# The order of three matmuls in a split-precision product with activations as stationary operand

## The chip, the cores and the metric

The kernel runs on one core of a Trainium2 chip. The metric is the device time of one execution in microseconds; the kernel before has a median of 1224.03 us over three runs.

## The reference

Two layers work on 512 tokens of width 1,024. The first mixes tokens by attention with forget gates, the second by a gated short convolution. Each is followed by an MLP with squared ReLU of width 4,096 and by a gated embedding. Everything is in 32-bit floats.

```python
for i in range(DEPTH):                                   # DEPTH = 2
    hn = rmsnorm(x, g[0])
    m = fox_attention(hn, ...) if i % 2 == 0 else short_conv(hn, ...)
    x = x + rmsnorm(m, g[1])
    f = jnp.square(jax.nn.relu(rmsnorm(x, g[2]) @ w_mlp_up[i])) @ w_mlp_down[i]
    x = x + rmsnorm(f, g[3])
    gate = jax.nn.sigmoid(rmsnorm(x, g[4]) @ w_ple_gate[i])
    x = x + rmsnorm((p[i] @ w_ple_proj[i]) * gate, g[5])
```

## The kernel before

TensorE multiplies in a reduced 32-bit format. To keep the precision, each operand is split in two parts: a high part (`hi`, a cast on ScalarE, line 272) and a low part (`lo`, the source less the high part, on VectorE or GpSimd, line 273). A product a x b is then three matmuls into the same PSUM bank: high by high, and the two mixed ones. The function `mm3` (line 262) issues them. Its first operand is the stationary one: it is loaded into the array ahead of each matmul. The second streams through, 512 columns at most. The reduction runs over blocks of 128 rows, so a bank gets a chain of such products; the first matmul of the chain clears the bank and the last one closes it.

Two kinds of calls exist. Where the result is to lie transposed (the projections `qk`, `up`, `u`, `c`, `b`), the weights are stationary and the tokens stream. Where it is to lie with tokens on the partitions, the activations of 128 tokens are stationary and 512 columns of weights stream. The second kind are the values `v`, the output projections `o` of attention and `co` of the convolution, the down projection `dn`, the gate `pg` and the embedding `pp`. `dn` sums its blocks in seven products per group by Strassen's scheme, with sums of activations (`A11`, `A12`, `S1`, `S3`, ...) as stationary operand.

Weights come from memory through 14 buffers (`raw`), fetched on SP's queue. `wide` returns the high and low part of a block and has up to eight further blocks prepared ahead, so `wh` and `wl` are normally ready long before their use. In names such as `wl_7264` the number tells one tile from the next. The activations' parts `hTh` and `hTl` are made after each norm: four transposes (`n_p`, line 320) into a bank, a cast to `hTh`, a subtraction to `hTl`. In the profile's rows a matmul reads out<-moving,stationary.

The order of instructions on each engine is set by a scheduler, which simulates the program and moves an instruction ahead where another would wait; at the start, at the end of attention and in the very last block some engines have an order by hand. Engines run their queues in order.

Of the kernel before, what the change touches and what calls it, by code (L numbers as in the profile page):

```python
# [21 lines left out]
KT = D // P  # L22
# [46 lines left out]
def trunk(ctx: ExitStack, tc, x, pT, g, wv, wqk, bf, wo, wci, wcq, cw, wco, wup, wdn, wpp, wpg, out):  # L69
    nc = tc.nc  # L70
# [122 lines left out]
    def wide(*key, soon=SOON):  # L193

        prepare(where[key] + 1 + soon)
        return ready[key]
# [62 lines left out]
        while any(k in keys for _, k, _ in later):  # L259
            later.pop(0)[2]()  # L260

    def mm3(ps, a, b, start, stop):

        nc.tensor.matmul(ps, a.hi, b.hi, start=start, stop=False)  # L264
        nc.tensor.matmul(ps, a.lo, b.hi, start=False, stop=False)  # L265
        nc.tensor.matmul(ps, a.hi, b.lo, start=False, stop=stop)  # L266
        streamed[0] += 3 * ps.shape[-1]
        due()

# [98 lines left out]
    def tokens_of(pair, t):  # L368
        return pair.at(lambda h: h[:, t * P : (t + 1) * P])

    def tokens(pair, k, t):
        return pair.at(lambda h: h[:, k, t * P : (t + 1) * P])

    def soon(t, n):

        return FEW if n else SOON

    def mixer_out(kind, lhs, xs, gB, then, opened):


        mgs, sums = {}, {}
        for t, n in BLOCKS:
            if (t, n) == (2, 0):
                prepare(where[kind, 1, KT - 1] + 1 + SOON)
            at = (t, n) in opened
            ps = opened.pop((t, n)) if at else bank(f"{kind}{n}_{t}")
            for k in range(KT - 1 if at else 0, KT):
                mm3(ps, lhs(k, t), wide(kind, n, k, soon=soon(t, n)), k == 0, k == KT - 1)
            sums[t, n] = squares(ps, f"{kind}s{n}_{t}")
            mgs[t, n] = gained(ps, gB, n, f"{kind}m{n}_{t}")  # L390
            if (t, 1 - n) in mgs:
                residual(t, *([d.pop((t, i)) for i in range(2)] for d in (mgs, sums)), xs[t],
                         f"{kind}r")
                then(t)

    def attention(hT, first_x, g0, b_f, work, by_hand):
# [47 lines left out]
        def values(c, t, mid=None):  # L444

            c0, width = V_CHUNKS[c]
            n_v = min(width, D - c0)
            ps = bank(f"v{c}_{t}")
            for k in range(KT):
                if width == 256:  # L450
                    w = wide("v", c, k // 2).at(lambda u: u[:, k % 2 * 256 : k % 2 * 256 + 256])
                else:
                    w = wide("v", c, k, soon=0 if mid else SOON)
                if not mid:
                    mm3(ps[:, :width], tokens(hT, k, t), w, k == 0, k == KT - 1)
            HH, LH, HL = ("hi", "hi"), ("lo", "hi"), ("hi", "lo")
            for n in range(2 if mid else 0):
                for part, of in (HH, HL, LH) if n == 0 else (HH, LH, HL):
                    if n and of == "lo":
                        mid()  # L460
                    for k in range(4 * n, 4 * n + 4):
                        nc.tensor.matmul(
                            ps[:, :width], getattr(tokens(hT, k, t), part),
                            getattr(ready["v", c, k], of),
                            start=k == 0 and part == of, stop=k == KT - 1 and of == "lo",
                        )

            def keep_v():
                if n_v < width:
                    nc.vector.tensor_tensor(  # L470
                        out=logit[:, t * H : (t + 1) * H], in0=ps[:, n_v:width], in1=b_f,
                        op=ALU.add,
                    )
                splits = []
                for c1 in range(0, n_v, 256):
                    src = ps[:, c1 : c1 + 256].rearrange("p (i e d) -> p i e d", e=2, d=HD)
                    block = vs[t][(c0 + c1) // 256].rearrange("p (i r) -> p i r", i=2)
                    for e in range(2):
                        hi = block[:, :, 192 * e : 192 * e + HD]
                        lo = block[:, :, 64 + 64 * e : 128 + 64 * e]  # L480
                        splits.append((hi, lo, src[:, :, e, :]))
                for hi, _, src in splits:
                    nc.scalar.copy(hi, src)
                for hi, lo, src in splits:
                    nc.vector.tensor_tensor(
                        out=lo, in0=src, in1=hi.bitcast(F32), op=ALU.subtract
                    )

            return keep_v
# [103 lines left out]
        banks_o = {}  # L593
        oT, complete, streaming = [], [], [True]
# [11 lines left out]
        def out_part(ts, ks):  # L606

            streaming.clear()
            split_o()
            for k in ks:  # L610
                for t in ts:
                    for n in range(2):
                        if (t, n) not in banks_o:
                            banks_o[t, n] = bank(f"o{n}_{t}")
                        w = wide("o", n, k, soon=O_SOON)
                        mm3(banks_o[t, n], tokens(oT[0], k, t), w, k == 0, False)
                        yield

        def stream():
# [29 lines left out]
        with tc.manual_schedule(engines={E.PE, E.DVE, E.Activation, E.Pool}):  # L649
# [3 lines left out]
            hs = scale_rows(0, r)  # L653
# [195 lines left out]
    def mlp(l, hT, xs, then, late):  # L849
# [45 lines left out]
        def down(gr, A):  # L895

            for i in STEPS:
                a_name, b_name = PRODUCTS[i]
                banks = [bank(f"dn{l}_{gr}_{i}{s}") for s in range(2)]
                for p in range(2):  # L900
                    w = wide("dn", l, gr, b_name, p)
                    for s in range(2):
                        mm3(
                            banks[s], A[a_name, p].at(lambda h: h[:, s * P : (s + 1) * P]), w,
                            p == 0, p == 1,
                        )
                for s in range(2):
                    if gr == 0:
                        acc[i, s] = page(f"acc{l}_{i}_{s}")
                        nc.scalar.copy(acc[i, s][:, :S], banks[s])  # L910
                    else:
                        a = acc[i, s][:, :S]
                        ins = nc.vector.tensor_tensor(out=a, in0=banks[s], in1=a, op=ALU.add)  # L913
                        if gr == 1:
                            tc.add_manual_dep(
                                ins.ins, lows[gr].ins.name,
                                mybir.DependencyInfo(
                                    mybir.DependencyClass.NoSync, mybir.DependencyReason.DATA
                                ),
                            )  # L920
# [25 lines left out]
        total, hs, gB = combine(), [], []  # L946
# [14 lines left out]
        for t in range(NB):  # L961
            banks = [bank(f"dn{l}_7_{t}_{n}") for n in range(2)]
            for f, n in [(f, n) for f in range(4) for n in range(2)] if t == 0 else [
                (f, n) for n in range(2) for f in range(4)
            ]:
                w = wide("dn", l, 7, n, f, soon=14)
                mm3(banks[n], tokens_of(hs[f], t), w, f == 0, f == 3)
            for n in range(2):
                a = total[t, n][:, :S]
                nc.vector.tensor_tensor(out=a, in0=banks[n], in1=a, op=ALU.add)  # L970
            fs = [total[t, n][:, :S] for n in range(2)]
            sums = [squares(f, f"fs{l}_{t}_{n}") for n, f in enumerate(fs)]
            mg = [gained(f, gB, n, None, total[t, n]) for n, f in enumerate(fs)]
            residual(t, mg, sums, xs[t], f"mr{l}")
            then(t)

    def ple(l, hT, xs, gB, then):
        def proj(t, n):
            pe = bank(f"pp{l}_{n}_{t}")
            for k in range(2):  # L980
                mm3(
                    pe, tokens_of(wide("p", l, k), t),
                    wide("pp", l, n, k), k == 0, k == 1,
                )
            return pe

        def last_block(t, n, gate, mg, q):
# [5 lines left out]
            for c, pe in zip(halves, pes):  # L993
                for k in range(2):
                    mm3(
                        pe[:, : S // 2], tokens_of(wide("p", l, k), t),
                        wide("pp", l, n, k).at(lambda w: w[:, c]), k == 0, k == 1,
                    )
            with tc.manual_schedule(engines={mybir.EngineType.DVE}):
                for i, (c, pe) in enumerate(zip(halves, pes)):  # L1000
# [13 lines left out]
                c = halves[1]  # L1014
# [24 lines left out]
        for t, n in BLOCKS:  # L1039
# [4 lines left out]
            ps = bank(f"pg{l}_{n}_{t}")  # L1044
            for k in range(KT):
                w = wide("pg", l, n, k, soon=soon(t, n))
                mm3(ps, tokens(hT, k, t), w, k == 0, k == KT - 1)
            gate = page(f"gate{l}_{n}_{t}")
            nc.scalar.activation(gate[:, :S], ps, AF.Sigmoid)
            if l == 1 and (t, n) == BLOCKS[-1]:  # L1050
# [42 lines left out]
    oT = lhs  # L1093
# [120 lines left out]
```

## Time and profile before

| | |
|---|---|
| three runs | 1223.32, 1224.03, 1225.0 us |
| the profiled execution | 1224.06 us, its span 1222.3 us |
| mean granted TensorE clock | 0.998 |
| TensorE busy | 1211.6 us (99%), 6,209 matmuls, as many loads of a stationary operand |
| VectorE, ScalarE, GpSimd busy | 913.6 (75%), 671.6 (55%), 666.0 us (54%) |

PE stands for the matmuls, PEld for the loads of the stationary operand, which run beside matmuls. A group's row gives line, engine, operation, operands and shape, the count, the busy time, the mean duration in ns and the idle time ahead. A row of the timeline gives the start, the duration and the same names. The printed ends of matmuls are modelled and overlap; the pace is read from the starts.

### The profile page before, as it was taken

What the parts mean: (1) busy time and instruction counts of PE and PEld (TensorE: products, weight loads), DVE (VectorE), ACT (ScalarE), POOL (GpSimd) and SP (SyncE); (2) the same over time, 40 slices, a digit from 0 to 9 for tenths busy, and PEclk for the clock granted to TensorE, in tenths of its full rate; (3) what the DMA queues carried; (4) which work ended last, traced back from release to release, by engine and by line L of the source; (5) the groups of instructions that cost most, each with busy time, mean ns of one, the idle gap of its engine ahead of it and who ended that gap; (6) DMA issues with size and microseconds to landing.
All of it is one profiled execution on the core that took longest, in us unless ns stands there. A gap on an engine that the chain in (4) does not pass through costs nothing.

```text
span 1222.3 us, 18723 instructions
## 1 busy us (share of the span) xinstructions
PE 1211.6 (99%) x6209; PEld 1033.0 (85%) x6209; DVE 913.6 (75%) x1420; ACT 671.6 (55%) x1421; POOL 666.0 (54%) x623
## 2 busy tenths in 40 slices
PE   9999999999999999999999999999999999999997
PEld 8888888898888888888889999989888888888886
DVE  6558888576769766879877798866776787669873
ACT  5457778558634563455565434445756345635551
POOL 5026667154887777775213255316677878778210
PEclk9999999999999999999999999999999999999999
DMA  8556554623244224428123033552422443235401
GB/s 275 156 154 164 167 146 127 207 87 104 79 137 127 90 70 128 138 80 291 64 91 114 19 103 98 162 172 70 138 79 61 137 138 98 66 114 182 163 14 56
DMA packets 86021, 148.73 MB, mean 122 GB/s; under 512 B 10082, under 2 KB 17810, under 8 KB 85924
## 3 DMA queue, kind: packets, MB, share of 16 engines
q1 hardware_dynamic: 85488, 147.01, 39.9%
q8 instruction: 49, 0.80, 0.3%
q10 hardware_dynamic: 436, 0.53, 0.1%
q14 instruction: 48, 0.39, 0.1%
HBM read 136.93 MB, written 6.37 MB: 117 GB/s over the span
## 4 chain that ended last, share of the span: by engine, by line
PE 94%; issue 2%; DVE 1%; ACT 1%; POOL 1%; DMA 0%; POOLq 0%; DVEq 0%; ACTq 0%
PE up L265 9%; PE up L266 9%; PE up L264 9%; PE dn L264 8%; PE dn L265 8%; PE dn L266 8%; PE qk L265 2%; PE qk L264 2%; PE qk L266 2%; PE pg L265 2%; PE pg L264 2%; PE pg L266 2%; PE pT L562 1%; PE n_p L320 1%; PE co L264 1%
## 5 line engine op out<-in xcount | busy, mean ns | idle before, releaser
L273 DVE TENSOR_TENSOR wl<-raw,wh 128x512 fp32r<-128x512 f32 (+1 forms) x387 | 377.2, 1018 | 14.7 <-ACT wh L272 13.3
L272 ACT CAST wh<-raw 128x512 fp32r<-128x512 f32 (+1 forms) x398 | 217.5, 620 | 4.6 <-DVE xd L356 4.4
L265 PE MATMUL up<-hTh,wl 128*128 128x512 f32 (+1 forms) x576 | 210.2, 365 | 0.0
L266 PE MATMUL up<-hTl,wh 128*128 128x512 f32 (+1 forms) x576 | 209.6, 365 | 0.0
L264 PE MATMUL up<-hTh,wh 128*128 128x512 f32 (+1 forms) x576 | 208.7, 366 | 0.0
L867 ACT ACTIVATE r<-up 128x512 f32<-128x512 f32 (+1 forms) x72 | 39.4, 547 | 203.9 <-PE up L266 191.1
L273 POOL TENSOR_TENSOR wl<-dn_T,wh 128x512 fp32r<-128x512 f32 x96 | 132.5, 1413 | 30.0 <-ACT wh L272 30.0
L167 POOL TENSOR_TENSOR dn_T<-raw,raw 128x512 f32<-128x512 f32 x56 | 86.4, 1553 | 70.1 <-DMA raw<-in_wdn 61.2
L265 PEld LDWEIGHTS up<-hTh,wl 128*128 128x128 f32 x576 | 108.6, 189 | 17.5
L264 PEld LDWEIGHTS up<-hTh,wh 128*128 128x128 f32 x576 | 108.6, 189 | 17.5
L266 PEld LDWEIGHTS up<-hTl,wh 128*128 128x128 f32 x576 | 108.3, 189 | 17.5
L913 DVE TENSOR_TENSOR acc<-dn,acc 128x512 f32<-128x512 f32 x168 | 107.4, 679 | 15.4 <-PE dn L266 15.4
L167 POOL TENSOR_TENSOR dn_T<-raw,dn_T 128x512 f32<-128x512 f32 x56 | 92.3, 1649 | 2.2
L272 ACT CAST wh<-dn_T 128x512 fp32r<-128x512 f32 x112 | 61.4, 616 | 11.0 <-POOL dn_T L167 11.0
L273 DVE TENSOR_TENSOR A12l<-q,A12h 128x512 fp32r<-128x512 f32 x28 | 22.5, 803 | 54.2 <-ACT A12h L272 54.2
L927 POOL TENSOR_TENSOR acc<-acc,acc 128x512 f32<-128x512 f32 x28 | 46.9, 1707 | 9.9 <-DVE acc L913 9.9
L265 PE MATMUL qk<-hTh,wl 128*128 128x512 f32 x128 | 51.0, 399 | 0.0
L266 PE MATMUL qk<-hTl,wh 128*128 128x512 f32 x128 | 51.0, 398 | 0.0
L264 PE MATMUL qk<-hTh,wh 128*128 128x512 f32 x128 | 50.9, 398 | 0.0
L265 PE MATMUL pg<-wh,hTl 128*128 128x512 f32 x128 | 50.5, 394 | 0.0
L264 PE MATMUL pg<-wh,hTh 128*128 128x512 f32 x128 | 50.4, 394 | 0.0
L266 PE MATMUL pg<-wl,hTh 128*128 128x512 f32 x128 | 50.1, 392 | 0.0
(403 smaller groups left out, 3213.4 us busy)
## 6 DMA issues: line engine op xcount, KB each, us to landing
raw<-in_wup SPq DMA_DIRECT2D x128, 256.0 KB, 2.8
raw<-in_wdn SPq DMA_DIRECT2D x128, 256.0 KB, 2.9
raw<-in_wcq SPq DMA_DIRECT2D x36, 256.0 KB, 3.0
raw<-in_wqk SPq DMA_DIRECT2D x32, 256.0 KB, 4.6
raw<-in_wpg SPq DMA_DIRECT2D x32, 256.0 KB, 4.1
g<-in_g SPq DMA_DIRECT2D x22, 256.0 KB, 5.5
prl<-neg_c SPq DMA_DIRECT2D x16, 256.0 KB, 6.8
raw<-in_wo SPq DMA_DIRECT2D x16, 256.0 KB, 3.3
```

What stands on the lines that cost most here:

```text
L167: ins = nc.gpsimd.tensor_tensor(out=B[name], in0=B[a], in1=B[b], op=op)
L264: nc.tensor.matmul(ps, a.hi, b.hi, start=start, stop=False)
L265: nc.tensor.matmul(ps, a.lo, b.hi, start=False, stop=False)
L266: nc.tensor.matmul(ps, a.hi, b.lo, start=False, stop=stop)
L272: nc.scalar.copy(hi, src)
L273: return eng.tensor_tensor(out=lo, in0=src, in1=hi.bitcast(F32), op=ALU.subtract)
L320: nc.tensor.transpose(ps[:, j * P : (j + 1) * P], h[:, j * P : (j + 1) * P], ident)
L562: nc.tensor.transpose(ps[:, b * P : (b + 1) * P], probs[h][b][:, j * P : (j + 1) * P], ident)
L867: nc.scalar.activation(r[:, :n], ps[:, :n], AF.Relu)
L913: ins = nc.vector.tensor_tensor(out=a, in0=banks[s], in1=a, op=ALU.add)
L927: nc.gpsimd.tensor_tensor(out=a, in0=a, in1=acc[i, s][:, :S], op=ALU.add)
```

## The change

The calls with activations as stationary operand pass a flag, and `mm3` then issues the two mixed products in the other order: the weights' low part second, with the stationary operand of the first matmul, and the activations' low part third. The calls with weights as stationary operand keep their order.

```diff
-    def mm3(ps, a, b, start, stop):
-
+    def mm3(ps, a, b, start, stop, turned=False):
+
+        last = (a.hi, b.lo), (a.lo, b.hi)
         nc.tensor.matmul(ps, a.hi, b.hi, start=start, stop=False)
-        nc.tensor.matmul(ps, a.lo, b.hi, start=False, stop=False)
-        nc.tensor.matmul(ps, a.hi, b.lo, start=False, stop=stop)
+        nc.tensor.matmul(ps, *last[not turned], start=False, stop=False)
+        nc.tensor.matmul(ps, *last[turned], start=False, stop=stop)
...
-                mm3(ps, lhs(k, t), wide(kind, n, k, soon=soon(t, n)), k == 0, k == KT - 1)
+                mm3(ps, lhs(k, t), wide(kind, n, k, soon=soon(t, n)), k == 0, k == KT - 1, True)
...
-                mm3(ps, tokens(hT, k, t), w, k == 0, k == KT - 1)
+                mm3(ps, tokens(hT, k, t), w, k == 0, k == KT - 1, True)
```

The same `True` is added to the calls for `v`, `o`, `dn` (twice) and `pp` (twice). The lines of the changed kernel stand one further down: 265, 266 and 267 for the three matmuls.

The first place is PE at the end of attention, where the output product of attention (`o`) is put between the products of the last heads (`ps_o`, `sc`). Before:

```order
L264 MATMUL o_0_2921<-wh_3086,hTh 128x512
L265 MATMUL o_0_2921<-wh_3086,hTl 128x512
L580 MATMUL ps_o_3134<-ph_0_3070,v_3_153 128x512
L581 MATMUL ps_o_3134<-pl_0_3071,v_3_153 128x512
L580 MATMUL ps_o_3134<-ph_1_3099,v_3_157 128x384
L266 MATMUL o_0_2921<-wl_3087,hTh 128x512
L546 MATMUL sc_2_3137<-kh_1_2621,qs_1_2620 128x384
```

The same place after the change:

```order
L265 MATMUL o_0_2921<-wh_3086,hTh 128x512
L581 MATMUL ps_o_3134<-ph_0_3070,v_3_153 128x512
L582 MATMUL ps_o_3134<-pl_0_3071,v_3_153 128x512
L581 MATMUL ps_o_3134<-ph_1_3099,v_3_157 128x384
L266 MATMUL o_0_2921<-wl_3087,hTh 128x512
L267 MATMUL o_0_2921<-wh_3086,hTl 128x512
L547 MATMUL sc_2_3137<-kh_1_2621,qs_1_2620 128x384
```

The three matmuls of attention still stand ahead of the one with `wl_3087`; the one with `hTl` has gone behind it.

The second place is PE in the gate product of the first layer, second column of weights, first block of tokens (`pg_1_0`). Before:

```order
L264 MATMUL pg_1_0_7395<-wh_7263,hTh 128x512
L265 MATMUL pg_1_0_7395<-wh_7263,hTl 128x512
L320 MATMUL n_p_0_7426<-ident,n_h_0_7199 128x128 x4
L266 MATMUL pg_1_0_7395<-wl_7264,hTh 128x512
L264 MATMUL pg_1_0_7395<-wh_7272,hTh 128x512
```

After:

```order
L265 MATMUL pg_1_0_7395<-wh_7263,hTh 128x512
L321 MATMUL n_p_0_7426<-ident,n_h_0_7199 128x128 x4
L266 MATMUL pg_1_0_7395<-wl_7264,hTh 128x512
L267 MATMUL pg_1_0_7395<-wh_7263,hTl 128x512
L265 MATMUL pg_1_0_7395<-wh_7272,hTh 128x512
```

The transposes follow the first matmul directly, and the one with `wl_7264` comes one matmul sooner. Some rows later the four transposes `n_p_1_7433` likewise move ahead of the matmul with `wl_7291`.

The third place is VectorE beside it. Before:

```order
L273 TENSOR_TENSOR wl_7264<-raw_7265,wh_7263 128x512
L273 TENSOR_TENSOR wl_7273<-raw_7274,wh_7272 128x512
L273 TENSOR_TENSOR wl_7282<-raw_7283,wh_7281 128x512
L273 TENSOR_TENSOR wl_7291<-raw_7292,wh_7290 128x512
L273 TENSOR_TENSOR hTl<-n_p_0_7426,hTh 128x4x128
L273 TENSOR_TENSOR wl_7300<-raw_7301,wh_7299 128x512
```

After:

```order
L274 TENSOR_TENSOR wl_7264<-raw_7265,wh_7263 128x512
L274 TENSOR_TENSOR wl_7273<-raw_7274,wh_7272 128x512
L274 TENSOR_TENSOR wl_7282<-raw_7283,wh_7281 128x512
L274 TENSOR_TENSOR hTl<-n_p_0_7426,hTh 128x4x128
L274 TENSOR_TENSOR wl_7291<-raw_7292,wh_7290 128x512
L274 TENSOR_TENSOR wl_7300<-raw_7301,wh_7299 128x512
```

The subtraction for `hTl` goes ahead of the one for `wl_7291`; the others keep their places.

More of the change, by code (lines that the diff above doesn't have):

```diff
@@ L454, in values @@
                 if not mid:
-                    mm3(ps[:, :width], tokens(hT, k, t), w, k == 0, k == KT - 1)
+                    mm3(ps[:, :width], tokens(hT, k, t), w, k == 0, k == KT - 1, True)
             HH, LH, HL = ("hi", "hi"), ("lo", "hi"), ("hi", "lo")
@@ L615, in out_part @@
                         w = wide("o", n, k, soon=O_SOON)
-                        mm3(banks_o[t, n], tokens(oT[0], k, t), w, k == 0, False)
+                        mm3(banks_o[t, n], tokens(oT[0], k, t), w, k == 0, False, True)
                         yield
@@ L904, in down @@
                             banks[s], A[a_name, p].at(lambda h: h[:, s * P : (s + 1) * P]), w,
-                            p == 0, p == 1,
+                            p == 0, p == 1, True,
                         )
@@ L966, in mlp @@
                 w = wide("dn", l, 7, n, f, soon=14)
-                mm3(banks[n], tokens_of(hs[f], t), w, f == 0, f == 3)
+                mm3(banks[n], tokens_of(hs[f], t), w, f == 0, f == 3, True)
             for n in range(2):
@@ L982, in proj @@
                     pe, tokens_of(wide("p", l, k), t),
-                    wide("pp", l, n, k), k == 0, k == 1,
+                    wide("pp", l, n, k), k == 0, k == 1, True,
                 )
@@ L996, in last_block @@
                         pe[:, : S // 2], tokens_of(wide("p", l, k), t),
-                        wide("pp", l, n, k).at(lambda w: w[:, c]), k == 0, k == 1,
+                        wide("pp", l, n, k).at(lambda w: w[:, c]), k == 0, k == 1, True,
                     )
```

## The prediction

> **What bounds the kernel now.** I read the page first: the engines' busy time, the clock over the slices and the chain of work that ended last.
>
> ```profile
> span 1222.3 us, 18723 instructions
> PE 1211.6 (99%) x6209; PEld 1033.0 (85%) x6209; DVE 913.6 (75%) x1420; ACT 671.6 (55%) x1421; POOL 666.0 (54%) x623
> PEclk9999999999999999999999999999999999999999
> PE 94%; issue 2%; DVE 1%; ACT 1%; POOL 1%; DMA 0%; POOLq 0%; DVEq 0%; ACTq 0%
> ```
>
> TensorE is busy in 99% of the span at full clock, and 94% of the chain lies on it. A busy PE is not yet a PE at its peak, so two questions follow: how far apart the matmuls start, and how long PE waits. The timeline of PE in a dense stretch of the MLP answers the first. The rows are the first and last of ten consecutive matmuls with 512 columns, and of seven with 256 columns.
>
> ```profile
> 300.47 0.39 PE L264 MATMUL up<-hTh,wh 128*128 128x512 f32 x1
> ...
> 302.51 0.39 PE L264 MATMUL up<-hTh,wh 128*128 128x512 f32 x1
> 279.55 0.28 PE L266 MATMUL up<-hTl,wh 128*128 128x256 f32 x1
> ...
> 280.27 0.28 PE L266 MATMUL up<-hTl,wh 128*128 128x256 f32 x1
> ```
>
> Nine steps in 2.04 us are 0.2267 us a matmul of 512 columns; six steps in 0.72 us are 0.120 us for 256. The second 256 columns cost 0.107 us, so about 0.013 us of each matmul (2 x 0.120 - 0.2267) does not depend on its width. The durations printed (0.39) overlap and say nothing of the pace. The view of waits, for PE alone, answers the second question.
>
> ```profile
> PE warm_p L1083 <- DVE warm L1066: 1.6, 1, 1.6
> PE ps_o L580 <- DVE pl L273: 0.9, 1, 0.9
> PE c L264 <- DVE za L803: 0.7, 1, 0.7
> PE pT L562 <- DVE pl L273: 0.6, 1, 0.6
> ```
>
> That is the whole answer: 3.8 us in four waits, none of them in a product that the change touches. `warm_p` is the start, `ps_o` and `pT` are attention's own, and `c` has the weights stationary. So the change works inside a stream that hardly ever stops. It can gain only by a faster pace, and lose by a new wait.
>
> **The change part by part.** Every product that is turned keeps its three matmuls, its operands and its sum in PSUM. Nothing is added or removed on any engine: 6,053 rows on PE, 1,403 on DVE, 1,256 on ACT, 621 on POOL and 613 on SP before and after. There are 774 turned products of 512 columns: 456 of `dn`, 128 of `pg`, 64 each of `o` and `co`, 32 of `v`, 30 of `pp`. Another 36 have 256 columns. Three things can differ.
>
> *The pace.* In a turned product the first two matmuls now share their stationary operand; before, they shared the moving one. The rows of two forms of `dn` show what the shared moving operand was worth, and the loads of a pair that already shares its stationary operand (`qs`, lines 546 and 547) show whether the second load is left out.
>
> ```profile
> L265 PE MATMUL dn<-wh,S3l 128*128 128x512 f32 x112 | 43.6, 389 | 0.0
> L266 PE MATMUL dn<-wl,S3h 128*128 128x512 f32 x112 | 40.0, 389 | 0.0
> L546 PEld LDWEIGHTS sc<-kh,qs 128*128 128x128 f32 x64 | 12.1, 189 | 2.0 <-DVE nmx L549 0.3 <-DVE pl L273 0.3
> L547 PEld LDWEIGHTS sc<-kl,qs 128*128 128x128 f32 x64 | 12.1, 188 | 1.3
> ```
>
> The second matmul of a `dn` product repeats the moving operand of the first, the third repeats neither: both have 389 ns. The 64 second matmuls on `qs` have 64 loads of their own, of 188 ns like every other. What such a pair costs in an undisturbed stretch is in the timeline at 79 us.
>
> ```profile
> 79.31 0.39 PE L266 MATMUL qk<-hTl,wh 128*128 128x512 f32 x1
> 79.55 0.39 PE L546 MATMUL sc<-kh,qs 128*128 128x512 f32 x1
> 79.55 0.19 PEld L547 LDWEIGHTS sc<-kl,qs 128*128 128x128 f32 x1
> 79.77 0.39 PE L547 MATMUL sc<-kl,qs 128*128 128x512 f32 x1
> 79.78 0.19 PEld L264 LDWEIGHTS qk<-hTh,wh 128*128 128x128 f32 x1
> 80.00 0.39 PE L264 MATMUL qk<-hTh,wh 128*128 128x512 f32 x1
> ```
>
> From the first `sc` matmul to the second, with the same stationary operand, it is 0.22 us; from the second to the `qk` matmul after it, with another one, 0.23. The load runs beside the matmul ahead of it, whatever it loads. I take 0.00 us a pair. The reading is good to 0.01 us, so the bound from these rows is 774 x 0.01 = 7.7 us either way; I put it among the rivals and not into the likeliest case, because the pair sits on the ordinary pace.
>
> The Trainium skill ("TensorE: Matmul & The Clock Gate", Part 2, on loading the stationary operand) speaks for a gain: the load is an instruction of its own so that one can load once and multiply repeatedly. The rows at 79 us disagree for this kernel: the load is issued again. By the rule the time would be that of the first rival below; by the rows the pace adds 0.
>
> *The wait for the weights' low part.* It is needed one matmul earlier, the activations' low part one later. In most places the weights are split far ahead. Two places are tight. The first is the end of attention, where VectorE makes the low part of the output weights (`wl_3087` of the order) just in time.
>
> ```profile
> 207.53 0.40 PE L265 MATMUL o<-wh,hTl 128*128 128x512 f32 x1
> 207.76 0.43 PE L580 MATMUL ps_o<-ph,v 128*128 128x512 f32 x1
> 208.03 0.40 PE L581 MATMUL ps_o<-pl,v 128*128 128x512 f32 x1
> 208.26 0.34 PE L580 MATMUL ps_o<-ph,v 128*128 128x384 f32 x1
> 208.44 0.39 PE L266 MATMUL o<-wl,hTh 128*128 128x512 f32 x1
> 207.55 0.69 DVE L273 TENSOR_TENSOR wl<-raw,wh 128x512 fp32r<-128x512 f32 x1
> ```
>
> The low part is done at 207.55 + 0.69 = 208.24. The new order keeps the three attention matmuls between the first and the second of this product; only the 0.23 us matmul at 207.53 goes from ahead of them to behind. So the waiting matmul comes up at 208.44 - 0.23 = 208.21: 0.03 us early. Behind it on PE wait the activations' low part, which is ready, and the next scores. Before, a gap of 0.20 us was enough, so the wait is between 0.03 and 0.23 us; I take 0.15. The later products of this kind have more room and are costed at nothing.
>
> The second place is the gate product of the second column (`pg_1_0`), in both layers, where VectorE works without a pause.
>
> ```profile
> 608.82 0.39 PE L265 MATMUL pg<-wh,hTl 128*128 128x512 f32 x1
> 609.05 0.60 PE L320 MATMUL n_p<-ident,n_h 128*128 128x128 f32 x4
> 609.40 0.47 PE L266 MATMUL pg<-wl,hTh 128*128 128x512 f32 x1
> ...
> 611.33 0.39 PE L265 MATMUL pg<-wh,hTl 128*128 128x512 f32 x1
> 607.93 2.49 DVE L273 TENSOR_TENSOR wl<-raw,wh 128x512 fp32r<-128x512 f32 x4
> 609.68 0.59 ACT L272 CAST hTh<-n_p 128x512 fp32r<-128x512 f32 x1 [0.31 <-PE n_p L320]
> 610.34 0.68 DVE L273 TENSOR_TENSOR hTl<-n_p,hTh 128x512 fp32r<-128x512 f32 x1
> 610.94 1.88 DVE L273 TENSOR_TENSOR wl<-raw,wh 128x512 fp32r<-128x512 f32 x3
> ```
>
> Four low parts in 2.49 us are 0.62 us each, so the first (`wl_7264`) is done at 608.55 and needed, after the move, at 609.40 - 0.23 = 609.17: 0.6 us to spare. The fourth (`wl_7291`) is done at 610.42; the new order puts the `hTl` of 0.68 us ahead of it, so it is done by 611.1. The order also puts four transposes (0.35 us, from 609.05 to 609.40 for such a group) ahead of its matmul, which then starts at 611.33 + 0.35 = 611.68: again 0.6 us to spare. Less is left if `hTl` has to wait for ScalarE's cast of the transposes, which ends 0.23 us sooner than before at best, at 609.68 + 0.59 - 0.23 = 610.04: then `wl_7291` ends at 610.04 + 0.68 + 0.62 = 611.34, 0.35 us ahead. I cost the place at nothing; its cover is these 0.35 to 0.6 us, twice in the run.
>
> *The stalls that are there.* The clearest in a turned product are in the first group of `dn`, by the timeline of PE.
>
> ```profile
> 285.63 0.39 PE L266 MATMUL dn<-wl,A12h 128*128 128x512 f32 x1
> 285.99 0.50 PE L264 MATMUL dn<-wh,S1h 128*128 128x512 f32 x1
> ...
> 287.29 0.40 PE L266 MATMUL dn<-wl,S1h 128*128 128x512 f32 x1
> 287.81 1.19 PE L264 MATMUL dn<-wh,A12h 128*128 128x512 f32 x4
> ```
>
> Against the pace they lose 0.36 - 0.23 = 0.13 and 0.52 - 0.23 = 0.29 us. Both fall on the first matmul of a product (line 264), which waits for a high part or a free bank, and the first stays first. Nothing is recovered: 0. The few swaps on DVE and ACT and one on SP follow the shifted matmuls by one or two instructions; the tightest of them is the `pg_1_0` case above.
>
> The sum is +0.15 us. The profiled execution took 1224.06 us, 1.8 more than its span; the median of the three runs is 1224.03. So **1224.2 us**: no change that can be measured, 0.2% (2.4 us) being about what a measurement of this kernel can tell from none.
>
> **The rivals.** *A shared stationary operand makes the pace faster.* If all of the 0.013 us that each matmul costs beyond its columns were the exchange of the stationary operand, and fell away where it stays, 774 + 36 products would save 810 x 0.013 = 10.5 us: 1213.7. For it: the change makes exactly such pairs in 810 places. Against it: the loads of `qs` are issued all the same, and the pair keeps the pace. Smaller gains down to 1221.6 belong here: 3% for the full effect, 5% for a part.
>
> *VectorE becomes the bound in the gate product (slower).* The low parts are now awaited one matmul sooner, with `hTl` ahead of one. The point from which it decides is 0.35 us of lateness. If two more VectorE operations than I count (2 x 0.62 us) fell ahead of the awaited low part, PE would stand 1.24 - 0.35 = 0.9 us a layer; with three, 1.5 us. Two layers and the 0.15 give 1226.0 and 1227.2. For it: VectorE has no pause from 607.93 to 612.82. Against it: the order moves one operation, not three. 7% for over 1226.5.
>
> *A wait that is there goes away (faster).* Transposes behind a product's first matmul start 0.23 us sooner and could shorten the 0.9 and 0.6 us that `ps_o` and `pT` wait in attention's end. If both vanished, 1224.2 - 1.5 = 1222.7, still within 0.2%. Against it: the 0.9 us falls at 219 us, after a stretch of PE work that is not shortened. 10%.
>
> **How the numbers follow.** The forecast has 75%; with the rival of 1222.7, 85% lie within 0.2%. Faster by more has 8% (the pace), slower by more 7% (VectorE). The range takes the bounds: below, 1.5 us of vanished waits and the 0.7 us by which the runs lay under their median (1223.32), 1224.2 - 2.2 = 1222.0; above, 0.08 us more at the end of attention, 0.9 us for one layer late by two operations and 1.0 us for the runs' spread upward (1225.0): 1226.2.
>
> **What would show it.** Right: PE's list of waits again holds these four, PE starts 512-column matmuls every 0.2267 us in `dn`, with as many loads as matmuls, and VectorE's low parts in `pg_1_0` end before their matmul. Wrong: fewer loads than matmuls, or a step under 0.22 us from the first to the second matmul of a turned product, or a PE wait for `wl` in `pg` or `o`.

## The result, and the profile after

The change makes the kernel slower by a little. Six runs after it took 1227.12 to 1229.44 us, median 1229.11; six of the kernel before on the same chip 1223.32 to 1225.0, median 1224.22. The ratio is 1.0037, with a 95% interval of 1.0026 to 1.0047: 4.9 us, outside the forecast range (1222.0 to 1226.2). The profiled execution took 1228.79 us.

The page of the profile after: the span, the engines and the chain.

```profile
span 1227.1 us, 18716 instructions
PE 1213.8 (99%) x6209; PEld 1032.9 (84%) x6209; DVE 917.4 (75%) x1420; ACT 671.6 (55%) x1421; POOL 669.5 (55%) x623
PE 89%; issue 3%; DVE 3%; ACT 2%; POOL 2%; DMA 0%; POOLq 0%; DVEq 0%; ACTq 0%
```

There are as many loads as matmuls, as before: no load is left out. But the chain lies on PE for 89% in place of 94%, and more of it on VectorE, ScalarE and GpSimd (1% each before). PE's waits after:

```profile
PE warm_p L1084 <- DVE warm L1067: 1.6, 1, 1.6
PE c L265 <- DVE za L804: 1.1, 1, 1.1
PE co L265 <- ACT wh L273: 1.1, 1, 1.1
PE ps_o L581 <- DVE pl L274: 0.9, 1, 0.9
PE c L266 <- DVE wl L274: 0.6, 1, 0.6
PE pT L563 <- DVE pl L274: 0.6, 1, 0.6
PE c L265 <- ACT wh L273: 0.2, 1, 0.2
```

Three are new, for a high or low part of weights, and none lies in `o` or `pg`. The list adds 2.3 us to the 3.8 of before, less than is lost. So I lined up the matmuls of the two traces by their place on PE and read how far the later one lags. The lag stays between 0.064 and 0.066 us from 300 to 595 us, over 602 matmuls of `dn`, and between 4.717 and 4.719 us from 880 to 1140 us, over 525 more. Nearly all of it comes in at three places (times of the trace before): **2.65 us** at 657 to 671 us (first block of the convolution), **1.39 us** at 790 us (its output projection `co`) and **0.61 us** at 855 us (first group of `dn`, layer 1). From 604 us to the end that is 4.68 us.

**The first place** begins 45 us earlier, on ScalarE at the first gate of layer 0. Before, then after:

```profile
610.17 1.66 ACT L272 CAST wh<-raw 128x512 fp32r<-128x512 f32 x3
611.85 1.28 ACT L1049 ACT_TABLE_LOAD   x1
613.14 0.60 ACT L1049 ACTIVATE gate<-pg 128x512 f32<-128x512 f32 x1
613.63 0.58 ACT L272 CAST hTh<-n_p 128x512 fp32r<-128x512 f32 x1
```

```profile
609.98 1.66 ACT L273 CAST wh<-raw 128x512 fp32r<-128x512 f32 x3
612.02 0.59 ACT L273 CAST hTh<-n_p 128x512 fp32r<-128x512 f32 x1 [0.38 <-PE n_p L321]
612.51 0.62 ACT L273 CAST wh<-raw 128x512 fp32r<-128x512 f32 x1
613.14 1.28 ACT L1050 ACT_TABLE_LOAD   x1
614.44 0.60 ACT L1050 ACTIVATE gate<-pg 128x512 f32<-128x512 f32 x1
```

These are the transposes of my second place, those that moved ahead of the matmul with `wl_7291`. With them the cast of `hTh` has gone ahead of the sigmoid's table load, and ScalarE waits 0.38 us for the transposes before it can make that cast; as many casts `wh<-raw` (204 from the start) stand ahead of the load as before. The gate starts 1.30 us later, while PE has lost nothing. The Trainium skill ("TensorE: Matmul & The Clock Gate", Part 1, on the array's architecture) says that ScalarE and VectorE work their queues strictly first in, first out; the trace agrees: the load (1.28 us) needs nothing from the transposes and starts 1.29 us later behind their cast.

From here a serial chain runs to the end of the stage: gate, product `e`, its square, the norm's factor on GpSimd, residual `xd`, the next square, `n0b_h`, and again for each block of tokens. It fell 1.1 us further behind at its third block of tokens, where two casts of `hTh` moved from behind the gate to ahead of it. ScalarE before, then after:

```profile
641.55 0.62 ACT L1049 ACTIVATE gate<-pg 128x512 f32<-128x512 f32 x1
642.04 1.10 ACT L272 CAST hTh<-n0b_p 128x512 fp32r<-128x512 f32 x2
642.99 0.68 ACT L295 ACTIVATE junk<-e 128x512 f32<-128x512 f32 x1
```

```profile
641.92 1.06 ACT L273 CAST hTh<-n0b_p 128x512 fp32r<-128x512 f32 x2
...
643.93 0.64 ACT L1050 ACTIVATE gate<-pg 128x512 f32<-128x512 f32 x1
...
645.46 0.73 ACT L296 ACTIVATE junk<-e 128x512 f32<-128x512 f32 x1
```

The gate is 2.38 us late, the square of `e` 2.47. VectorE at the chain's end and PE behind it, before and after:

```profile
655.63 1.42 DVE L311 SCALAR_TENSOR_TENSOR n0b_h<-xd,n0b_r_y,g 128x512 f32<-128x512 f32 x2 [1.98 <-POOL n0b_r_y L290]
656.96 4.07 DVE L273 TENSOR_TENSOR wl<-raw,wh 128x512 fp32r<-128x512 f32 x3
658.83 0.36 PE L265 MATMUL c<-hTh,wl 128*128 128x256 f32 x1
```

```profile
658.33 1.42 DVE L312 SCALAR_TENSOR_TENSOR n0b_h<-xd,n0b_r_y,g 128x512 f32<-128x512 f32 x2 [2.26 <-POOL n0b_r_y L291]
659.66 4.08 DVE L274 TENSOR_TENSOR wl<-raw,wh 128x512 fp32r<-128x512 f32 x3
660.40 0.39 PE L266 MATMUL c<-hTh,wl 128*128 128x256 f32 x1 [0.61 <-DVE wl L274]
671.27 0.39 PE L265 MATMUL c<-hTh,wh 128*128 128x256 f32 x1 [1.12 <-DVE za L804]
```

The low parts that the convolution starts with are queued behind the last `n0b_h`, 2.70 us later than before, and so are ScalarE's first weight casts there (654.46 and 657.16). PE loses 1.5 us up to the first matmul with a low part, 0.7 in smaller steps by 667 us, and 0.45 at 671 us, where it waits longer for `za`: 2.65 in all. The chain had next to no slack, although none of its engines is busy all the time and PE's list of waits had shown nothing of it before.

**The second place**, ScalarE in `co`, before and after, and PE after:

```profile
788.15 0.61 ACT L272 CAST wh<-raw 128x512 fp32r<-128x512 f32 x1
789.96 0.60 ACT L295 ACTIVATE junk<-co 128x512 f32<-128x512 f32 x1 [1.19 <-PE co L266]
```

```profile
792.89 0.60 ACT L296 ACTIVATE junk<-co 128x512 f32<-128x512 f32 x1 [2.32 <-PE co L267]
793.48 0.61 ACT L273 CAST wh<-raw 128x512 fp32r<-128x512 f32 x1
```

```profile
794.14 1.21 PE L265 MATMUL co<-wh,yh 128*128 128x512 f32 x4 [1.06 <-ACT wh L273]
```

A weight cast has gone behind a square that itself waits for PE to finish a block. PE then waits for the cast. **The third place** took the experiments to explain.

### The profile page after: what moved, and what is told of

Same layout as the page of the kernel before. It is cut to its first block, busy times and chain, and to the rows that moved or that the text cites. A ratio compares the mean times of both kernels' runs of the same rounds, so it can differ in the third digit from the quotient of the medians.

```text
span 1227.1 us, 18716 instructions
## 1 busy us (share of the span) xinstructions
PE 1213.8 (99%) x6209; PEld 1032.9 (84%) x6209; DVE 917.4 (75%) x1420; ACT 671.6 (55%) x1421; POOL 669.5 (55%) x623
## 4 chain that ended last, share of the span: by engine, by line
PE 89%; issue 3%; DVE 3%; ACT 2%; POOL 2%; DMA 0%; POOLq 0%; DVEq 0%; ACTq 0%
PE up L267 9%; PE up L266 9%; PE up L265 9%; PE dn L265 8%; PE dn L266 8%; PE dn L267 8%; PE qk L266 2%; PE qk L265 2%; PE qk L267 2%; PE pg L265 1%; PE pg L266 1%; PE pg L267 1%; PE pT L563 1%; PE n_p L321 1%; PE o L265 1%
## 5 line engine op out<-in xcount | busy, mean ns | idle before, releaser
L274 DVE TENSOR_TENSOR A11l<-q,A11h 128x256 fp32r<-128x256 f32 x28 | 23.0, 820 | 36.1 <-ACT A11h L273 36.1
```

The costliest lines, as they stand in the source:

```text
L274: return eng.tensor_tensor(out=lo, in0=src, in1=hi.bitcast(F32), op=ALU.subtract)
```

## The experiments

Theory 1: the turned matmuls cost nothing; what costs is that the scheduler, timing them anew, moved other instructions. Theory 2: the turned products cost by themselves. Theory 3: a gain from the shared stationary operand is there, but covered up.

Two kinds of edit are used. `turned` is given to some calls only, or to none. Or an edge holds one instruction behind another in its engine's queue; it sets the issue order and adds no wait between engines:

```diff
+    for after, first in HOLDS:
+        tc.add_manual_dep(
+            marks[after].ins, marks[first].ins.name,
+            mybir.DependencyInfo(mybir.DependencyClass.NoSync, mybir.DependencyReason.DATA),
+        )
```

Each run's list of pairs, which the kernels write into the head of this loop, is called `HOLDS` here. `marks` keeps instructions by name, for instance `("n40", 3, 1, "hi")`: the cast of `hTh` after the norm ahead of layer 0's gate, for the fourth block of tokens, second half. The table has the runs, with the median less that of the kernel before on the same chip, the ratio, and what each trace lost against the trace of before at the three places and in all from 604 us on. By 604 us the traces lie between 1.6 us ahead of the one before and 1.1 us behind it, also where nothing is turned up to there; the medians carry this, and these sums do not.

| run | median less before, us | ratio (95%) | 604 to 680 us | 785 to 800 | 800 to 880 | sum, us |
|---|---|---|---|---|---|---|
| after | +4.9 | 1.0037 (1.0026 to 1.0047) | 2.64 | 1.39 | 0.62 | 4.7 |
| rest | -0.1 | 1.0001 (0.9992 to 1.0010) | 0.33 | 0.00 | 0.01 | 0.3 |
| pg0 | +2.9 | 1.0022 (1.0013 to 1.0031) | 2.66 | 0.00 | 0.00 | 2.7 |
| edge | +3.5 | 1.0031 (1.0020 to 1.0042) | 3.53 | 0.00 | -0.02 | 3.6 |
| held_gate | +2.0 | 1.0017 (1.0009 to 1.0026) | 0.69 | 1.36 | 0.69 | 2.7 |
| co | +1.5 | 1.0013 (1.0004 to 1.0022) | 0.05 | 1.36 | 0.67 | 2.1 |
| co_wh1 | +1.3 | 1.0010 (1.0001 to 1.0019) | 0.04 | 0.00 | 0.69 | 0.7 |
| co_cor | +1.7 | 1.0015 (1.0006 to 1.0024) | 0.04 | 1.36 | 0.60 | 2.0 |
| co_st | +2.8 | 1.0026 (1.0017 to 1.0035) | 0.05 | 1.36 | 1.50 | 2.9 |
| co_all | +0.9 | 1.0007 (0.9998 to 1.0016) | 0.03 | 0.00 | 0.82 | 0.9 |
| co_pe1 | +0.4 | 1.0006 (0.9997 to 1.0015) | 0.00 | 0.00 | 0.25 | 0.3 |
| co_pe | -0.3 | 0.9998 (0.9989 to 1.0007) | 0.02 | 0.00 | -0.42 | -0.4 |
| held | +6.9 | 1.0058 (1.0045 to 1.0070) | 0.68 | 0.00 | 7.05 | 7.7 |
| held2 | +1.0 | 1.0006 (0.9997 to 1.0015) | 0.69 | 0.00 | 0.57 | 1.3 |
| held4 | +0.9 | 1.0012 (1.0003 to 1.0021) | 0.66 | 0.00 | 0.82 | 1.5 |
| held6 | +1.3 | 1.0008 (0.9999 to 1.0017) | 0.62 | 0.00 | 0.28 | 0.9 |
| held8 | +0.3 | 1.0003 (0.9995 to 1.0012) | 0.29 | 0.00 | -0.37 | -0.1 |

### Do the turned products cost, or gain?

**rest**: all turned but the gate of layer 0 and `co`.

```diff
-                mm3(ps, lhs(k, t), wide(kind, n, k, soon=soon(t, n)), k == 0, k == KT - 1, True)
+                mm3(ps, lhs(k, t), wide(kind, n, k, soon=soon(t, n)), k == 0, k == KT - 1, kind == "o")
...
-                mm3(ps, tokens(hT, k, t), w, k == 0, k == KT - 1, True)
+                mm3(ps, tokens(hT, k, t), w, k == 0, k == KT - 1, l == 1)
```

> All products are turned except the gate product of layer 0 and the convolution's output projection: 682 of 810. Theory 1: ScalarE and VectorE keep their order at the two places that lost time, so 1224.2 us, within 0.05% of the kernel before. Theory 2 (a cost of each turned product): 4.9 x 682 / 810 = 4.1 us, 1228.3 us, ratio 1.0034. A gain from the shared stationary operand would show here as a time below 1223.5 us.

682 turned products leave the time where it was, and PE's waits are the four of before, two of them a little longer (`za`, by 0.3 us at 668 us, is the whole loss in the table):

```profile
PE warm_p L1084 <- DVE warm L1067: 1.6, 1, 1.6
PE c L265 <- DVE za L804: 1.0, 1, 1.0
PE ps_o L581 <- DVE pl L274: 0.9, 1, 0.9
PE pT L563 <- DVE pl L274: 0.8, 1, 0.8
```

So theories 2 and 3 are out: no cost or gain per product can be seen, neither way.

### The first place: one cast ahead of one table load

**pg0**: only the gate of layer 0 is turned (`l == 0` in `pg`, `False` elsewhere).

> Only the 64 products of the gate in layer 0 are turned. Theory 1: the order of ScalarE and VectorE there is that of the full change, so 2.65 us are lost at 657 to 671 us and nothing elsewhere: 1224.6 + 2.65 = 1227.2 us, ratio 1.0022. Theory 2: 64 of 810 products, 0.4 us: 1225.0 us, ratio 1.0003.

**edge**: nothing is turned.

```diff
+    HOLDS = [("gate0_0_0", ("n40", 3, 1, "hi"))]
```

> No product is turned. One edge is added to the kernel before: in the first gate block of layer 0 ScalarE takes the cast of hTh ahead of the sigmoid with its table load, as it does after the change. The scheduler then also gives the later swaps of that stage by itself. Theory 1 (the order of ScalarE's queue costs the time, not the matmuls): the gate starts near 614.5 us instead of 613.1, the chain gate, square, norm, cast runs 2.4 to 2.7 us late at 650 us, and PE loses about 2.65 us in the first block of the convolution: 1224.2 + 2.65 = 1226.9 us, ratio 1.0022. Theory 2 (turned matmuls cost by themselves): nothing is turned, so 1224.2 us, ratio 1.0000.

**held_gate**: all turned, and the gate first again.

```diff
+    HOLDS = [(("n40", 3, 1, "hi"), "gate0_0_0"), (("n40", 3, 1, "lo"), "e0_0_0")]
```

> All products are turned as in the change; one pair of edges keeps the cast of hTh behind the first gate of layer 0 on ScalarE, and the subtraction for hTl behind that gate's product on VectorE, as before the change. Theory 1: the 2.65 us at 657 to 671 us come back, the rest (1.4 us at 790, 0.6 us at 855) stays: 1229.1 - 2.65 = 1226.5 us, ratio to the kernel before 1.0018. Theory 2: the edges change nothing on TensorE, so 1229.1 us, ratio 1.0040.

64 turned products make the whole first loss (2.66 us), and one edge on ScalarE makes a loss at the same place with none turned. ScalarE and PE of edge:

```profile
611.65 0.59 ACT L273 CAST hTh<-n_p 128x512 fp32r<-128x512 f32 x1 [1.05 <-PE n_p L324]
612.26 1.28 ACT L1053 ACT_TABLE_LOAD   x1
613.55 0.60 ACT L1053 ACTIVATE gate<-pg 128x512 f32<-128x512 f32 x1
```

```profile
614.20 0.50 PE L265 MATMUL pg<-wh,hTh 128*128 128x512 f32 x1 [0.96 <-ACT gate L1053]
```

At this point the execution is 1.22 us ahead of the profile of before, so the gate at 613.55 answers to 614.77 there, 1.63 us late. I had expected 1.3 to 1.4 us and 2.65 us in all. It is not the same loss in every part: in edge the transposes have not moved on PE, so the cast waits 1.05 us for them in place of 0.38, and the gate comes so late that PE also waits 0.96 us for the gate to read its bank. 1.30 us are lost there and 2.24 in the convolution, 3.5 in all. In held_gate the later swaps of the stage go away by themselves, and 2.0 of the 2.65 us come back. The other 0.69 us are 0.35 at 613 us and 0.34 at 668 us.

### The second and third place

**co**: only `co` is turned. **co_wh1**: with it, the first square behind the weight cast again.

```diff
+    HOLDS = [("cos0_0", ("co", 1, 0, "hi"))]
```

> Only the 64 products of the convolution's output projection are turned. Theory 1: the scheduler moves one cast of a weight block behind a square on ScalarE, and casts of hTh ahead of the last statistics; 1.4 us at 790 us and 0.6 us in the first dn group of layer 1 are lost, nothing at 657 us: 1224.2 + 2.0 = 1226.2 us, ratio 1.0016, with the PE wait of 1.1 us for wh. Theory 2 (a cost of each turned product): 64 of 810 products, 4.9 x 64 / 810 = 0.4 us: 1224.6 us, ratio 1.0003.

> Only the convolution's output projection is turned, and one edge keeps the first square of it on ScalarE behind the cast of the weight block that it had overtaken. Theory 1: the wait of 1.1 us for wh at 790 us is gone and 1.36 us come back; the 0.7 us in the first dn group of layer 1 stay: 1226.1 - 1.36 = 1224.7 us, ratio 1.0002 to 1.0006. Theory 2: 1226.1 us as without the edge.

Both came as theory 1 has it: co loses 1.36 and 0.67 us, and the one edge gives the 1.36 back.

For the 0.67 us I first held the queues of VectorE (**co_cor**), ScalarE (**co_st**), and both with the edge of co_wh1 (**co_all**) in the order of before:

```diff
+    HOLDS = [(("cor", 2, 1), "com0_2")]
```

> Only the convolution's output projection is turned, and one edge keeps on VectorE the residual xd of the second column behind the gain product com, which it had overtaken while it still had to wait for the norm's factor from GpSimd. Theory 1a (this wait at the head of VectorE's queue makes the last norm late): the 0.66 us at 855 us come back, the 1.36 us at 790 us stay: 1225.5 us, ratio 1.0011. Theory 1b (ScalarE's casts ahead of the square do it): 1226.1 us, with 0.66 us still lost at 855 us.

```diff
+    HOLDS = [(("n21", 1, 0, "hi"), "n21_q0_2"), (("n21", 1, 1, "hi"), "n21_q0_2")]
```

> Only the convolution's output projection is turned, and two edges keep the casts of hTh for one block of tokens behind the square for the next block's statistics on ScalarE, as before the change. Theory 1: the wait of 1.1 us for wh at 790 us stays, and the 0.7 us at 855 us come back: 1226.1 - 0.7 = 1225.4 us, ratio 1.0007 to 1.0011; the trace is to show the norm chain of the last block no later than TensorE. A rival for the 0.7 us (the square is not what delays that chain, but VectorE's order of xd and wl): they stay, 1226.1 us.

> Only the convolution's output projection is turned, with the three kinds of edges that belong to it together (weight cast ahead of the first square, com ahead of xd, square ahead of two casts of hTh). Theory 1: 1.36 and 0.66 us come back, 1224.6 us, ratio 1.0000. Rival: 0.66 us stay at 855 us, 1225.3 us.

All three missed: 0.60, 0.66 and 0.65 us stayed at 855 us, and co_st lost 0.84 us more and co_all 0.17, since PE now waited for the `hTh` or `hTl` held back. What was left was the order of PE itself. Where the second column's first weights come in, the scheduler draws products of a later block ahead: five before the change (the fifth with two of its three matmuls), six after. With that, the block ahead of it (fourth block of tokens, second column) ends at row 4213 of PE's order in place of 4209, four matmuls or 0.9 us later, and the norm that waits for it comes 0.6 us later. **co_pe1** holds the sixth product back, **co_pe** the rest of the fifth too; both keep the edge of co_wh1.

```diff
+    HOLDS = [("cos0_0", ("co", 1, 0, "hi")), (("co", 2, 0, 5, 0), ("co", 3, 1, 7, 2))]
```

> Only the convolution's output projection is turned, with two edges: its first square behind the weight cast, and on TensorE the sixth product of the next block behind the last of the block before it. ScalarE's order is then that of the kernel before in full. Theory 1c: nothing is lost at 790 us and nothing (0.0 to 0.2 us) at 855 us: 1224.6 us, ratio 1.0000. Rival: 0.6 us at 855 us, 1225.3 us.

```diff
+    HOLDS += [(("co", 2, 0, 4, 1), ("co", 3, 1, 7, 2)), (("co", 2, 0, 4, 2), ("co", 3, 1, 7, 2))]
```

> Only the convolution's output projection is turned, with the edge for the weight cast and those on TensorE of held8: the block ends at row 4208. Theory 1c (the loss at 855 us follows the row at which that block ends: 0.66 us at 4213, 0.3 us at 4210, 0 at 4209): nothing lost at 855 us, 1224.6 us, ratio 1.0000. Rival (something else in the turned order): 0.3 us stay as in co_pe1.

The loss at 855 us follows the row at which that block ends: 0.57 to 0.69 us at row 4213, 0.25 and 0.28 at 4210 (co_pe1, held6), and at 4208 a gain of 0.42 (co_pe, held8). The traces bear the rows out: the block's end is the 158th of the 192 matmuls of `co` before, the 162nd after, the 159th in co_pe1 and the 157th in co_pe. So co_pe does not restore the order of before but improves on it. What carries the loss is GpSimd's first sum of weights for `dn`, which waits for the last norm. Before, after and co_pe:

```profile
833.57 2.53 POOL L167 TENSOR_TENSOR dn_T<-raw,raw 128x512 f32<-128x512 f32 x2 [1.58 <-DVE n_h L311]
```

```profile
838.30 2.54 POOL L167 TENSOR_TENSOR dn_T<-raw,raw 128x512 f32<-128x512 f32 x2 [1.58 <-DVE n_h L312]
```

```profile
831.43 2.51 POOL L167 TENSOR_TENSOR dn_T<-raw,raw 128x512 f32<-128x512 f32 x2 [1.58 <-DVE n_h L318]
```

After the change it is 4.73 us later while PE is 4.11 us late there, so 0.62 us on its own account; in co_pe it is 2.14 us earlier while PE is 1.54 us early, so 0.60 us earlier. The last `n_h` lies 0.63 us later and 0.60 earlier in the same count.

### All products turned, the queues held

**held** holds 23 pairs at the three places, **held2** the two pairs of held_gate and one each of co_wh1 and co_cor, **held4** also those of co_st, **held6** the first three and the one of co_pe1, **held8** those of co_pe, with this pair on top:

```diff
+    HOLDS += [(("n40", 3, 0, "hi"), ("pg", 0, 1, 4, "hi")), (("n40", 3, 0, "lo"), ("pg", 0, 1, 4, "lo"))]
```

> All 810 products are turned. Edges keep the order of ScalarE and VectorE of the kernel before at the three places that lost time: around the first gate of layer 0 and its residuals, at the first squares of the convolution's output projection, and at that projection's last norms. Theory 1 (queue order): all 4.7 us come back, 1224.6 us, ratio 1.0000 within 0.1%. Theory 2 (turned matmuls cost by themselves): nothing or little comes back, 1228 to 1229 us. Theory 3 (a shared stationary operand makes the pace faster, covered up by the queue order so far): under 1222.5 us.

> All 810 products are turned, with four edges in place of the many of the run held: the cast of hTh behind the first gate of layer 0 (and hTl behind that gate's product), the first square of the convolution's output projection behind the weight cast that it had overtaken, and on VectorE one residual (xd, second column of the third block) behind the gain product (com) that it had overtaken. The casts of hTh at the projection's end are left free, since holding them cost 5.3 us in the run held. Theory 1: no wait for wl at 660, for wh at 790 or for hTh at 825 us, 0.3 to 0.6 us left from the wait for za at 668 us and small swaps: 1224.4 to 1224.8 us, ratio 1.0002 to 1.0005. Theory 2 (turned matmuls cost by themselves): 1228 us or more.

> All 810 products are turned, with the edges of the run held2 and those of the run co_st together: first gate of layer 0 ahead of the cast of hTh, first square of the convolution's output projection behind its weight cast, on VectorE com ahead of the residual xd, on ScalarE the square for the next statistics ahead of two casts of hTh. Theory 1 (at the projection's end both the residual on VectorE and the square on ScalarE have to be on time, either alone leaves 0.6 us): the 0.58 us at 855 us come back too and no wait for hTh stands at 825 us: 1225.6 - 0.6 = 1225.0 us, ratio 1.0002, interval holding 1. Rival (the 0.6 us belong to the turned order itself, as each edge alone left them): 1225.6 us with 0.58 us lost at 855 us.

> All 810 products are turned, with four edges: the cast of hTh (and hTl) behind the first gate of layer 0, the first square of the convolution's output projection behind its weight cast, and, in place of the edges on VectorE and ScalarE at that projection's end, one on TensorE: the sixth product of the next block (third block of tokens, first column) stays behind the last product of the block before it. With it the orders of ScalarE and VectorE at the projection's end return by themselves. Theory 1c (the scheduler drew that product ahead, the block before it ended 0.9 us later on TensorE, and its norm with it): the 0.6 us at 855 us come back, and the time is 1225.0 us, ratio 1.0002 to 1.0005 with 0.6 us left at 613 and 668 us. Rival (the 0.6 us belong to the turned products themselves): 0.6 us still lost at 855 us, 1225.6 us.

> All 810 products are turned. As held6, with two more pairs of edges: around the first gate of layer 0 the first cast of hTh too stays behind the weight cast that it had overtaken, and on TensorE the rest of the fifth product of the next block stays behind the block before it as well, so that this block ends one row earlier than in the kernel before (row 4208 against 4209; 4213 after the change, 4210 in held6). Theory 1: nothing lost at 613 us and nothing at 855 us, 0.3 us left at 668 us: 1224.7 us, ratio 1.0000 to 1.0005. Rival (turned products cost by themselves): no better than held6, 1225.6 us.

held was wrong the other way. ScalarE held two casts of `hTh` behind a square that waited for a residual until 829.47 us, and PE waited for them:

```profile
PE up L265 <- ACT hTh L273: 5.3, 1, 5.3
```

An order that cost nothing in one program cost 5.3 us in the next, whose PE order differs. held2 and held4 left the third loss, as the co runs had; held6 halved it. In held8 next to nothing is left: its sum is -0.1 us, 4.8 us better than the change alone with every product turned, and at 613 us next to nothing is lost (0.05), so the 0.35 us there were the first cast of `hTh` ahead of a weight cast. 0.24 us at 668 us, a longer wait for `za`, stay and were not followed up. The 0.37 gained at the third place are not the change's own: co_pe, with the same edges there, has them with 64 products turned. Against co_pe, held8 is 0.3 us behind. PE's waits in held8:

```profile
PE warm_p L1090 <- DVE warm L1073: 1.6, 1, 1.6
PE c L266 <- DVE za L810: 0.9, 1, 0.9
PE ps_o L587 <- DVE pl L277: 0.9, 1, 0.9
PE pT L569 <- DVE pl L277: 0.6, 1, 0.6
```

No version is faster than the kernel before by more than the measurement can tell; co_pe, at 0.9998, is the nearest.

## Why the prediction was wrong

**The step that failed** is the last one of its sum: "The few swaps on DVE and ACT and one on SP follow the shifted matmuls by one or two instructions; the tightest of them is the `pg_1_0` case above." I costed them at nothing by looking for PE waits in the turned products. Swaps on ScalarE at two places cost 2.65 and 1.39 us, and a move on PE that the step does not name 0.61. What was wrong in the reading:

- The swaps on ScalarE got no rows of their own, as if an engine that is busy for 55% had room. The rows of `n0b_h` show that idle time there belongs to a chain that runs through ScalarE, GpSimd and VectorE in turn: at its end 2.70 us of lateness became 2.65 us on PE.
- The term for `pg_1_0` looked at PE and VectorE. On PE it was right: at 650 us the lag is where it was at 604 us, and over the same product in layer 1 it grows by 0.03 us. The same shift of the transposes moved a cast ahead of the table load on ScalarE, a queue that I did not follow to its end.
- PE's order moved by more than the swaps I listed: the block in `co` that ends four rows later was among them (0.61 us), and is neither a swap within a product nor on DVE or ACT.

**What held.** The pace is worth 0: over 602 matmuls of turned `dn` products the lag changes by no more than 0.002 us. I had left 8% for a gain; rest and held8 show none. The waits of `ps_o` and `pT` stayed (0.9 and 0.6 us). As many loads as matmuls are issued. The one term that was not 0, 0.15 us at the end of attention, came to nothing: `wl_3087` is done at 207.42 + 0.70 = 208.12 us and its matmul starts at 208.30, 0.17 behind the one ahead of it, as before; the lag, 0.03 us greater at 209 us, is back by 211. The sign of being right failed, as three waits joined the four. But no wait for `wl` in `pg` or `o` came up, so the signs that I named as "wrong" would not have shown the loss: they watched the turned products alone.

**A term that could have had a sign.** "Nothing is recovered" for the stalls in the first `dn` group, 0.13 + 0.29 us, was read in layer 0, where 0.08 us more were lost. The same group in layer 1 has stalls of its own: after the change it lost 0.61 us there, and co_pe and held8 gained 0.42 us and show no such step any more. That stall hung on the norm ahead of it, not on the order of the three matmuls.

**The rivals.** The slower one had the right place, the gate product of layer 0, and the wrong engine: not VectorE's low parts but ScalarE's table load. With 7% for slower, the chance was given to one mechanism; the reordering as such had no share of its own.

## What to carry to other kernels

When a scheduler sets the order, read its whole difference on every engine, and follow each swap to the next instruction that waits for something long: a table load, a square that waits for PE, a norm. An engine's idle time is slack only if what ends it is not the chain that the next stage starts from. To hold an order, find the one swap from which the others follow: in this kernel one pair of edges gave back 2.0 us, and 23 edges made the median worse by 2 us.

## What the runs showed of the hardware

- A cast held ahead of a table load of 1.28 us, with a wait of 1.05 us for the cast's transposes, cost 3.5 us (ratio 1.0031, 1.0020 to 1.0042) in a kernel where ScalarE is busy for 55% of the time.
- Whether the second matmul repeats the stationary or the moving operand of the first makes no difference to the pace that can be seen: no more than 0.002 us over 602 matmuls, with a load recorded for every matmul in both orders.
